# Two zero columns on three products of each block of 24

## The chip, the cores and the metric

The kernel runs on one core of a Trainium2 chip. What is measured is the time of one execution on the device, in microseconds. TensorE (PE in the profile, with its weight loads on a row of their own, PEld) multiplies; VectorE (DVE), ScalarE (ACT) and GpSimd (POOL) do the element-wise work; SyncE (SP) issues the transfers.

## The reference

Two transformer blocks on 256 tokens of width 1024, batch 1, in float32. The parts that matter here are the plain matrix products:

```python
def first_block(x, c, positions, w_ada, ...):
    ...
        proj = xn @ w_in[l]
        ...
        mixed = g_moba * (o_moba @ w_proj_moba[l]) + g_rwkv * (o_rwkv @ w_proj_rwkv[l])
        h = h + gt1 * (mixed @ w_out[l])
        xn2 = rms_norm(h, norm2_g[l]) * (1.0 + sc2) + sh2
        h = h + gt2 * peer_ffn(xn2, peer_wq[l], peer_subkeys[l], peer_u[l], peer_v[l])
...
def retrieve(args):                       # in peer_ffn
    ...
        hdn = jax.nn.gelu(jnp.einsum('cd,chkd->chk', xc, uc).astype(jnp.float32), approximate=False) * gc
        return jnp.einsum('chk,chkd->cd', hdn.astype(vc.dtype), vc)
...
def hybrid_layer(...):                    # second block: attention, then
    ...
    x = x + gate_f * ((jax.nn.silu(gt) * val) @ w_down)
```

The kernel computes the retrieval densely: all 16,384 experts' hidden values, with the gates of the chosen ones, and all their outputs.

## The kernel before, in words

**Products.** Every weight matrix is cut into units of 128 partitions by 1024 numbers, 512 KB each. `raw` loads a unit, and `wsplit` splits it into a rounded part `hi` (ScalarE, line 304) and the rest `lo` (VectorE, line 306), both in the type fp32r. The moving side is split in the same way into `xh` and `xl` (or `Hh` and `Hl`). A product of two float32 matrices then is three products: hi with xh, hi with xl, lo with xh. `mm3` writes them: first, for each of eight terms, hi·xh (line 322) and hi·xl (line 323), then eight times lo·xh (line 325). So a unit is a **block of 24** TensorE products, each with a weight load of 128x128 and 256 moving columns (the tokens).

**Two kinds of blocks.** In `t_unit` the eight terms are the eight rows k of `xh` (128 features each), and all 24 products add up in one PSUM tile `mmo`. In the two places with the outputs spread over 1024 columns (the experts' outputs, tiles `acc`, 128 units; the second block's down projection, tiles `facc`, 22 units), the eight terms are eight slices of the weights, the moving rows are one `Hh` and `Hl`, and each product adds into its own half of one of four PSUM tiles that stay open over all units.

**Stages in order of time.** The opening (to about 73 us) computes the first norm row by row and multiplies each row as it comes (`z`, lines 699 and 703). Then come the two mixers of block 1, its output projection (`wout` in `block1_out`, from 303 us), the query projection and the experts' hidden values (`u_pair`: two units into one PSUM tile; once the routing is known, from 550 us on, 16 small fp16 products `pg` follow most pairs), the experts' outputs (783 to 1141 us), block 2's mixer, its output projection (tiles `mh`, `ml`), and the feed-forward (1411 us to the end). At three of the norms `norm_apply` multiplies the first two units row by row (lines 457 and 465) while the rows are computed.

**Order.** All engines run their own instruction lists in order; the scheduler of the language layer has set that order at build time, from priorities and its own estimate of when operands are there. The waits are semaphores. `shim` allocates and clears small tiles so that the following tiles start at chosen addresses.

Of the kernel before, what the change touches and what calls it, by code (L numbers as in the profile page):

```python
# [269 lines left out]
class Prog:  # L270
    def __init__(self, tc, a, wu, cc, dbg=None, upto=99):
# [4 lines left out]
        self.nshim = 0  # L276
# [50 lines left out]
    def t_unit(self, u, xh, xl, kc=8):  # L327
        hi, lo = self.wsplit(u)
        hi, lo = hi.rearrange("p (k n) -> p k n", k=kc), lo.rearrange("p (k n) -> p k n", k=kc)
        ps = self.mm.tile([128, T], F32, name="mmo", tag="mm")  # L330
        A = slice(None)
        self.mm3([(ps, (A, k, slice(0, 128)), (A, k), k == 0, k == kc - 1) for k in range(kc)], hi, lo, xh, xl)
        return ps
# [297 lines left out]
    def block1_mixer(self):  # L631
# [5 lines left out]
        xh = bp.tile([128, 8, T], F32R, name="xh")  # L637
        xl = bp.tile([128, 8, T], F32R, name="xl")
# [401 lines left out]
    def block1_out(self):  # L1040
# [5 lines left out]
        xh = bp.tile([128, 8, T], F32R, name="xh")  # L1046
        xl = bp.tile([128, 8, T], F32R, name="xl")
# [19 lines left out]
    def peer(self):  # L1067
# [26 lines left out]
        xh = xp.tile([128, 8, T], F32R, name="xh")  # L1094
        xl = xp.tile([128, 8, T], F32R, name="xl")
# [127 lines left out]
        def u_pair(i):  # L1223
            ps = self.mm.tile([128, 2, T], F32, name="mmo", tag="mm")
            for j in range(2):
                hi, lo = self.wsplit(wu["u"] + i + j)
                hi, lo = hi.rearrange("p (k n) -> p k n", k=8), lo.rearrange("p (k n) -> p k n", k=8)
                A = slice(None)
                self.mm3([(ps[:, j], (A, k), (A, k), j == 0 and k == 0, k == 7) for k in range(8)], hi, lo, xh, xl)
# [90 lines left out]
        acc = [pa.tile([128, 2, T], F32, name=f"acc{i}") for i in range(4)]  # L1320
        from itertools import chain
        self.bg = chain(self.ada("ada1", "c", "b1", self.mod1, (5,), 24), self.ada("ada2", "c2", "b2", self.mod2, range(6)))
        for i in range(128):
            hi, lo = self.wsplit(wu["v"] + i)
            with tc.high_priority(self.lead + 12):
                Hh = vp.tile([128, T], F32R, name="Hh", bufs=4)
                Hl = vp.tile([128, T], F32R, name="Hl", bufs=4)
                self.split(hslice(i // 2 * 2)[:, i % 2], Hh, Hl)
            A = slice(None)
            self.mm3([(acc[d // 2][:, d % 2], (A, slice(d * 128, (d + 1) * 128)), A, i == 0 and d % 2 == 0, i == 127) for d in range(8)], hi, lo, Hh, Hl,  # L1330
                     inner=(i == 127))
# [19 lines left out]
    def block2_mixer(self):  # L1351
# [16 lines left out]
        xh = bp.tile([128, 8, T], F32R, name="xh")  # L1368
        xl = bp.tile([128, 8, T], F32R, name="xl")
# [345 lines left out]
    def ffn(self):  # L1715
# [4 lines left out]
        with ExitStack() as st:  # L1720
# [7 lines left out]
            xh = bp.tile([128, 8, T], F32R, name="xh")  # L1728
            xl = bp.tile([128, 8, T], F32R, name="xl")
# [8 lines left out]
            def up(i):  # L1738
# [12 lines left out]
                Hh = rp.tile([128, T], F32R, name="Hh", tag="Hh")  # L1751
# [36 lines left out]
```

## Time and profile before

| | |
|---|---|
| median of 3 runs | 1605.67 us (1603.52 to 1613.95) |
| the profiled execution, its own time | 1610.28 us |
| its span, first to last instruction | 1608.0 us |
| mean granted clock of TensorE | 0.996 |
| TensorE busy | 97% of the span, 13,022 products |
| VectorE, ScalarE busy | 79%, 63% |

A profile shows one execution, here the one with 1610.28 us: 4.6 us above the median of the other runs and inside their range. Busy time of TensorE is modelled from the starts of its products; since products overlap in the array, a single product is listed with some 0.28 us although the next one starts 0.11 to 0.12 us after it. What the engine delivers is read from the starts.

### The profile page before, as it was taken

Reading aid. Unit: us, or ns where it says so; the run is one execution under the profiler, and the core shown is the slowest. Engines: PE = TensorE matmul, PEld = TensorE weight load, DVE = VectorE, ACT = ScalarE, POOL = GpSimd, SP = SyncE. Lnnn points to the kernel's source line nnn. Section 1 sums busy time; section 2 is a strip of 40 time slices with the busy share of each in tenths; the row PEclk is TensorE's granted clock in tenths of the full one; section 3 lists DMA queues with packets and bytes.
Section 4 is the critical chain, followed back from the end, with each engine's and each line's share of the span. In section 5 each row is a group of like instructions: output and inputs, shape, how many; then the busy total and the mean of one; then the engine's idle time right before and its main releaser. Section 6 shows DMA issues by size and latency. Waiting matters only on the chain.

```text
span 1608.0 us, 33360 instructions
## 1 busy us (share of the span) xinstructions
PE 1562.9 (97%) x13022; PEld 1504.4 (94%) x13022; DVE 1263.5 (79%) x2731; ACT 1019.4 (63%) x2093; POOL 6.5 (0%) x43
## 2 busy tenths in 40 slices
PE   5999999999999999999999999999999999999998
PEld 5888898989999999999999999999888998989998
DVE  7887887878789777888877777777798986777776
ACT  4475765555545799998654445444679786665553
POOL 0000000000000000000000000000000000000000
PEclk8999999999999999999999999999999999999999
DMA  8632336645544544444688878788666322435553
GB/s 308 247 106 93 119 128 225 231 141 179 183 166 170 184 161 169 169 159 171 212 275 274 274 261 278 269 287 271 203 211 224 133 87 102 168 121 186 190 189 105
DMA packets 85261, 306.63 MB, mean 191 GB/s; under 512 B 9456, under 2 KB 10992, under 8 KB 84976
## 3 DMA queue, kind: packets, MB, share of 16 engines
q1 hardware_dynamic: 85104, 304.51, 55.4%
q8 instruction: 102, 1.67, 0.4%
q14 instruction: 55, 0.45, 0.1%
HBM read 303.42 MB, written 1.05 MB: 189 GB/s over the span
## 4 chain that ended last, share of the span: by engine, by line
PE 85%; DVE 8%; ACT 3%; DMA 2%; issue 1%; SPq 0%; DVEq 0%; ACTq 0%
PE mmo L322 14%; PE mmo L325 14%; PE mmo L323 14%; PE acc L322 7%; PE acc L323 7%; PE acc L325 7%; DVE lo L306 3%; DMA raw<-w 2%; PE pg L1263 2%; PE facc L322 1%; PE facc L325 1%; PE facc L323 1%; ACT hi L304 1%; PE pxt L893 1%; PE pz L881 1%
## 5 line engine op out<-in xcount | busy, mean ns | idle before, releaser
L304 ACT ACTIVATE hi<-raw 128x1024 fp32r<-128x1024 f32 (+1 forms) x465 | 490.4, 1057 | 370.0 <-PE mmo L323 136.1
L306 DVE TENSOR_TENSOR lo<-raw,hi 128x1024 fp32r<-128x1024 f32 (+1 forms) x465 | 565.2, 1218 | 165.7 <-ACT hi L304 162.6
L322 PE MATMUL mmo<-xh,hi 128*128 128x256 f32 x2032 | 498.8, 286 | 1.6 <-ACT hi L304 0.6
L323 PE MATMUL mmo<-xl,hi 128*128 128x256 f32 x2032 | 490.4, 281 | 0.0
L322 PEld LDWEIGHTS mmo<-xh,hi 128*128 128x128 f32 x2032 | 382.8, 189 | 5.7 <-ACT hi L304 2.1
L323 PEld LDWEIGHTS mmo<-xl,hi 128*128 128x128 f32 x2032 | 383.3, 189 | 1.9 <-issue 0.2
L325 PE MATMUL mmo<-xh,lo 128*128 128x256 f32 x2032 | 283.3, 281 | 4.7 <-DVE lo L306 4.6
L325 PEld LDWEIGHTS mmo<-xh,lo 128*128 128x128 f32 x2032 | 255.6, 189 | 7.2 <-DVE lo L306 6.5
L322 PE MATMUL acc<-Hh,hi 128*128 128x256 f32 x1024 | 241.8, 278 | 0.5 <-ACT Hh L363 0.5
L323 PE MATMUL acc<-Hl,hi 128*128 128x256 f32 x1024 | 241.0, 278 | 0.0
L322 PEld LDWEIGHTS acc<-Hh,hi 128*128 128x128 f32 x1024 | 192.3, 188 | 0.7 <-ACT Hh L363 0.7
L323 PEld LDWEIGHTS acc<-Hl,hi 128*128 128x128 f32 x1024 | 192.5, 188 | 0.1
L325 PE MATMUL acc<-Hh,lo 128*128 128x256 f32 x1024 | 139.4, 277 | 0.0
L325 PEld LDWEIGHTS acc<-Hh,lo 128*128 128x128 f32 x1024 | 127.3, 188 | 0.0
L388 DVE SCALAR_TENSOR_TENSOR acc<-raw,sil,acc 128x1024 f32<-128x1024 f32 x70 | 89.8, 1283 | 44.8 <-DMA raw<-w 44.7
L1245 ACT ACTIVATE D<-iota,i 128x128 f16<-128x128 f16 x256 | 84.6, 404 | 0.2
L1252 DVE TENSOR_TENSOR B<-O,iT 128x512 f16<-128x512 f16 x128 | 46.1, 417 | 0.0
L323 PE MATMUL facc<-Hl,hi 128*128 128x256 f32 x176 | 42.8, 281 | 0.0
L322 PE MATMUL facc<-Hh,hi 128*128 128x256 f32 x176 | 42.8, 281 | 0.0
L364 DVE TENSOR_TENSOR Hl<-hidA,Hh 128x256 fp32r<-128x256 f32 x96 | 40.0, 418 | 0.0
L363 ACT ACTIVATE Hh<-hidA 128x256 fp32r<-128x256 f32 x96 | 38.2, 400 | 0.0
L1246 ACT ACTIVATE A<-D 128x512 f16<-128x512 f16 x64 | 37.8, 628 | 0.0
(503 smaller groups left out, 2273.3 us busy)
## 6 DMA issues: line engine op xcount, KB each, us to landing
raw<-w SPq DMA_DIRECT2D x542, 512.0 KB, 4.1
aw<-w SPq DMA_DIRECT2D x16, 512.0 KB, 7.3
raw<-w SPq DMA_DIRECT2D x6, 384.0 KB, 3.3
whole<-w SPq DMA_DIRECT2D x4, 512.0 KB, 7.2
c<-w SPq DMA_DIRECT2D x3, 512.0 KB, 6.2
x<-xT SPq DMA_DIRECT2D x2, 512.0 KB, 5.7
hres<-xT SPq DMA_DIRECT2D x1, 1024.0 KB, 5.5
sk<-w SPq DMA_DIRECT2D x2, 512.0 KB, 5.6
```

What stands on the lines that cost most here:

```text
L304: self.s.activation(hi[:, :n], r[:, :n], AF.Copy)
L306: self.v.tensor_tensor(lo[:, :n], r[:, :n], hi[:, :n].bitcast(F32), OP.subtract)
L322: m(out, whi[w], xhi[x], start=start, stop=False, skip_group_check=True)
L323: m(out, whi[w], xlo[x], start=False, stop=False, skip_group_check=True)
L325: m(out, wlo[w], xhi[x], start=False, stop=stop, skip_group_check=True)
L363: self.s.activation(hi, src, AF.Copy)
L364: self.v.tensor_tensor(lo, src, hi.bitcast(F32), OP.subtract)
L388: v.scalar_tensor_tensor(acc, w, sc, acc, OP.mult, OP.add)
L1245: s.activation(D[:, j], iota, AF.Abs, bias=i1[:, t0 + j:t0 + j + 1])
L1246: s.activation(A, D, AF.Relu, scale=-1.0, bias=1.0)
L1252: v.tensor_tensor(B[p], O, row(1 + p), OP.mult)
L1263: mm(pg[:, j], B[p][:, :, j], A[:, j], start=(j + p == 0), stop=(j == 3 and p == 1), skip_group_check=True)
```

## The change

Each moving tile gets 64 more columns behind its last row, which GpSimd clears once (`rows`). In the blocks that use such a tile, three of the 24 products take 258 moving columns instead of 256: the last row and two of the zeros behind it. Their output is two columns wider, so that the zeros are added to two columns beyond the product's own, which are either unused (in `t_unit` the PSUM tile is two columns wider) or the beginning of the other half of the tile.

So that the wide products stand eight apart, `unit` starts each block with row 7 (hi·xh), puts hi·xl of row 7 in the ninth place and lo·xh of row 7 in the seventeenth. In `u_pair` the first unit of each pair has the wide products. `spread` does the same for `acc` and `facc` in the places 1, 9 and 17 of each block (slices 0 and 4 with hi, slice 0 with lo), all with the same moving row `Hh`; the last block is without. The four `Hh` tiles are now named ones, used in turn. The blocks that `t_units` writes, the second block's output projection (`mh`, `ml`) and the products of the opening and the norms keep 256 columns.

In all, 190 blocks of `mmo` (three in `xh`/`xl` each), 127 of `acc` and 21 of `facc` have wide products: 338 blocks, 1,014 products.

```diff
+    def rows(self, pool, k, name, **kw):
+        t = pool.tile([128, k * T + 64], F32R, name=name, **kw)
+        self.g.memset(t.bitcast(F32)[:, k * T:], 0.0)
+        x = t[:, :k * T].rearrange("p (k n) -> p k n", k=k)
+        return x, t[:, (k - 1) * T:k * T + 2]
+
+    def unit(self, ps, wide, hi, lo, xh, xl, kc, start=True):
+        tails, A, q = self.tails.get(id(xh)), slice(None), slice(0, 128)
+        ops = [(w, x, k) for k in range(kc) for w, x in ((hi, xh), (hi, xl))]
+        low = [(lo, xh, k) for k in range(kc)]
+        if tails and wide is not None and kc == 8:
+            a, b = ops[-2:]
+            ops = [a] + ops[:7] + [b] + ops[7:-2]
+            low = low[-1:] + low[:-1]
+        else:
+            tails = None
+        ops += low
+        for n, (w, x, k) in enumerate(ops):
+            if tails and k == kc - 1:
+                out, mv = wide, tails[0 if x is xh else 1]
+            else:
+                out, mv = ps, x[:, k]
+            self.pe.matmul(out, w[:, k, q], mv, start=start and n == 0, stop=n == len(ops) - 1, skip_group_check=True)
...
+    def spread(self, acc, hi, lo, Hh, Hl, wide, first, last):
+        C = lambda d: slice(d * 128, (d + 1) * 128)
+        if last:
+            ops = [(d, w, x) for d in range(8) for w, x in ((hi, Hh), (hi, Hl), (lo, Hh))]
+        else:
+            ops = [(d, w, x) for d in range(8) for w, x in ((hi, Hh), (hi, Hl))] + [(d, lo, Hh) for d in range(8)]
+        for n, (d, w, x) in enumerate(ops):
+            out = acc[d // 2][:, d % 2]
+            if n % 8 == 0 and not last:
+                out, x = acc[d // 2].rearrange("p j n -> p (j n)")[:, :T + 2], wide
+            self.pe.matmul(out, w[:, C(d)], x, start=first and d % 2 == 0 and w is hi and (n % 2 == 0), stop=last and w is lo, skip_group_check=True)
...
-        xh = bp.tile([128, 8, T], F32R, name="xh")
-        xl = bp.tile([128, 8, T], F32R, name="xl")
+        (xh, a), (xl, b) = self.rows(bp, 8, "xh"), self.rows(bp, 8, "xl")
+        self.tails[id(xh)] = a, b
...
-                self.mm3([(ps[:, j], (A, k), (A, k), j == 0 and k == 0, k == 7) for k in range(8)], hi, lo, xh, xl)
+                wide = ps.rearrange("p j n -> p (j n)")[:, :T + 2] if j == 0 else None
+                self.unit(ps[:, j], wide, hi, lo, xh, xl, 8, j == 0)
```

How the order of TensorE's instructions moves is seen at three places. The first is any block of the experts' outputs, here the first half of one. Before:

```order
L322 MATMUL acc_10720<-Hh,hi 128x256
L323 MATMUL acc_10720<-Hl,hi 128x256
L322 MATMUL acc_10720<-Hh,hi 128x256
L323 MATMUL acc_10720<-Hl,hi 128x256
L322 MATMUL acc_10721<-Hh,hi 128x256
L323 MATMUL acc_10721<-Hl,hi 128x256
L322 MATMUL acc_10721<-Hh,hi 128x256
L323 MATMUL acc_10721<-Hl,hi 128x256
L322 MATMUL acc_10722<-Hh,hi 128x256
```

Now, from the second product of a block on, to the ninth:

```order
L371 MATMUL acc_10726<-Hl,hi 128x256
L371 MATMUL acc_10726<-Hh_10734,hi 128x256
L371 MATMUL acc_10726<-Hl,hi 128x256
L371 MATMUL acc_10727<-Hh_10734,hi 128x256
L371 MATMUL acc_10727<-Hl,hi 128x256
L371 MATMUL acc_10727<-Hh_10734,hi 128x256
L371 MATMUL acc_10727<-Hl,hi 128x256
L371 MATMUL acc_10728<-Hh_10734,hi 128x258
```

Nothing has moved here; the first and the ninth product have 258 columns.

The second place is TensorE at the beginning of block 1's output projection. The products with `orh` and `orl` are the last of the branch projections, out of which `xh` is still being made, row by row up to row 7. Before, the first `wout` unit begins with row 0:

```order
L322 MATMUL mmo<-orh,hi 128x256
L323 MATMUL mmo<-orl,hi 128x256
L325 MATMUL mmo<-orh,lo 128x256 x4
L322 MATMUL mmo<-xh,hi 128x256
L323 MATMUL mmo<-xl,hi 128x256
L322 MATMUL mmo<-xh,hi 128x256
L323 MATMUL mmo<-xl,hi 128x256
```

Now, with row 7 first:

```order
L348 MATMUL mmo<-orh,hi 128x256
L349 MATMUL mmo<-orl,hi 128x256
L351 MATMUL mmo<-orh,lo 128x256 x4
L313 MATMUL mmo<-xh,hi 128x258
L313 MATMUL mmo<-xh,hi 128x256
L313 MATMUL mmo<-xl,hi 128x256
L313 MATMUL mmo<-xh,hi 128x256
L313 MATMUL mmo<-xl,hi 128x256
```

All products of the first units, which stood before those that need row 7, stand behind one that needs it.

The third place is TensorE at the end of the opening, before the last of its eight rows (products `z`). Before, 22 products of the next stage (`mmo`) stand between the seventh and the eighth row:

```order
L699 MATMUL z_122<-xh,lo 128x256 x2
L699 MATMUL z_123<-xh,lo 128x256 x2
L322 MATMUL mmo<-xh,hi 128x256
L323 MATMUL mmo<-xl,hi 128x256
L322 MATMUL mmo<-xh,hi 128x256
L323 MATMUL mmo<-xl,hi 128x256
```

Now the eighth row follows at once (the names z are counted two higher):

```order
L737 MATMUL z_124<-xh,lo 128x256 x2
L737 MATMUL z_125<-xh,lo 128x256 x2
L737 MATMUL z_122<-xh,hi 128x256 x2
L737 MATMUL z_123<-xh,hi 128x256 x2
L737 MATMUL z_124<-xh,hi 128x256 x2
L737 MATMUL z_125<-xh,hi 128x256 x2
```

The 22 products have moved behind the `z` of row 7, where all 48 of the next stage now stand together. In the same way, at the three norms with `norm_apply`, the places between the rows held 7 or 8 products of other units than the small ones and now hold 6.

## Rows read from the trace of the kernel before

**Rows 1.** The page, parts 1 and 4: busy times and the chain by engine

```profile
PE 1562.9 (97%) x13022; PEld 1504.4 (94%) x13022; DVE 1263.5 (79%) x2731; ACT 1019.4 (63%) x2093; POOL 6.5 (0%) x43
...
PE 85%; DVE 8%; ACT 3%; DMA 2%; issue 1%; SPq 0%; DVEq 0%; ACTq 0%
```

**Rows 2.** The page, part 5: one group of the feed-forward, busy and mean ns

```profile
L323 PE MATMUL facc<-Hl,hi 128*128 128x256 f32 x176 | 42.8, 281 | 0.0
```

**Rows 3.** Timeline, TensorE, experts' outputs: block starts 16 blocks apart (start, us, engine)

```profile
986.99 0.28 PE L322 MATMUL acc<-Hh,hi 128*128 128x256 f32 x1
...
1030.51 0.28 PE L322 MATMUL acc<-Hh,hi 128*128 128x256 f32 x1
```

**Rows 4.** Timeline, TensorE, an earlier stretch there: block starts 16 blocks apart

```profile
885.48 0.28 PE L322 MATMUL acc<-Hh,hi 128*128 128x256 f32 x1
...
930.70 0.28 PE L322 MATMUL acc<-Hh,hi 128*128 128x256 f32 x1
```

**Rows 5.** Windows, TensorE: stretch, length, busy (products), clock, DMA share, GB/s

```profile
388.91:407.40 18.49, 18.49 (x159) 1.00 0.43 148
...
494.68:515.63 20.95, 20.95 (x180) 1.00 0.45 155
883.00:933.00 50.00, 50.00 (x427) 1.00 0.80 268
1034.00:1085.00 51.00, 51.00 (x436) 1.00 0.82 279
...
1431.00:1600.00 169.00, 169.00 (x1437) 1.00 0.49 169
```

**Rows 6.** Timeline, TensorE, two pairs of hidden-value units with gate products between

```profile
551.41 0.28 PE L322 MATMUL mmo<-xh,hi 128*128 128x256 f32 x1
...
555.89 1.10 PE L325 MATMUL mmo<-xh,lo 128*128 128x256 f32 x8
...
557.93 0.28 PE L323 MATMUL mmo<-xl,hi 128*128 128x256 f32 x1
558.05 0.28 PE L322 MATMUL mmo<-xh,hi 128*128 128x256 f32 x1
...
558.28 0.28 PE L322 MATMUL mmo<-xh,hi 128*128 128x256 f32 x1
...
562.37 1.07 PE L325 MATMUL mmo<-xh,lo 128*128 128x256 f32 x8
```

**Rows 7.** Groups by line, TensorE: 985 to 1033 us, then block 2's mixer (1141 to 1391)

```profile
L323 PE MATMUL acc<-Hl,hi 128*128 128x256 f32 x142 | 33.1, 276 | 0.0
...
L325 PE MATMUL mmo<-xh,lo 128*128 128x256 f32 x288 | 39.5, 279 | 0.0
```

**Rows 8.** Timeline at the end of the opening: TensorE and, ahead of row 7, ScalarE

```profile
62.68 0.28 PE L322 MATMUL mmo<-xh,hi 128*128 128x256 f32 x1
...
64.17 0.51 ACT L438 ACTIVATE xh<-nt,mod 128x256 fp32r<-128x256 f32 x1 [3.53 <-DVE nt L437]
...
65.27 0.40 PE L699 MATMUL z<-xh,hi 128*128 128x256 f32 x2
```

**Rows 9.** Timeline at the start of block 1's output projection: TensorE and ScalarE

```profile
303.44 0.28 PE L322 MATMUL mmo<-xh,hi 128*128 128x256 f32 x1
...
306.65 0.50 PE L323 MATMUL mmo<-xl,hi 128*128 128x256 f32 x2
306.97 0.42 ACT L363 ACTIVATE xh<-gt 128x256 fp32r<-128x256 f32 x1 [1.72 <-DVE gt L1054]
307.44 0.51 PE L322 MATMUL mmo<-xh,hi 128*128 128x256 f32 x2 [0.28 <-ACT xh L363]
```

**Rows 10.** Windows, all engines, at the norm of 327 us (columns as in rows 5)

```profile
326.00:331.00 5.00, 2.33 (x12) 1.43 (x12) 3.17 (x6) 3.31 (x8) 0.00 (x0) 1.00 0.62 210
331.00:335.00 4.00, 4.00 (x18) 3.53 (x17) 2.92 (x8) 2.52 (x7) 0.00 (x0) 0.57 0.02 9
```

**Rows 11.** Timeline, TensorE, the same norm: a product put between the rows

```profile
331.58 0.42 PE L322 MATMUL mmo<-xh,hi 128*128 128x256 f32 x1
```

More of the change, by code (lines that the diff above doesn't have):

```diff
@@ L329, in t_unit @@
         hi, lo = hi.rearrange("p (k n) -> p k n", k=kc), lo.rearrange("p (k n) -> p k n", k=kc)
[L330 to L333, printed above, removed]
+        ps = self.mm.tile([128, T + 2], F32, name="mmo", tag="mm")
+        self.unit(ps[:, :T], ps, hi, lo, xh, xl, kc)
+        return ps[:, :T]
+    def spread(self, acc, hi, lo, Hh, Hl, wide, first, last):
[9 more added lines that the diff above has]
+            self.pe.matmul(out, w[:, C(d)], x, start=first and d % 2 == 0 and w is hi and (n % 2 == 0), stop=last and w is lo, skip_group_check=True)
     def t_units(self, hi, lo, kc, nbs, xh, xl, n, where=None):
@@ L1045, in block1_out @@
         sy.dma_start(h, self.a["xT"])
-        xh = bp.tile([128, 8, T], F32R, name="xh")
-        xl = bp.tile([128, 8, T], F32R, name="xl")
+        (xh, a), (xl, b) = self.rows(bp, 8, "xh"), self.rows(bp, 8, "xl")
+        self.tails[id(xh)] = a, b
         for j in range(4):
@@ L1320, in peer @@
         acc = [pa.tile([128, 2, T], F32, name=f"acc{i}") for i in range(4)]
+        Hhs = [(x[:, 0], w) for x, w in (self.rows(vp, 1, f"Hh{i}", tag=f"Hh{i}", bufs=1) for i in range(4))]
         from itertools import chain
@@ L1324, in peer @@
             hi, lo = self.wsplit(wu["v"] + i)
+            (Hh, wide), Hl = Hhs[i % 4], vp.tile([128, T], F32R, name="Hl", bufs=4)
             with tc.high_priority(self.lead + 12):
-                Hh = vp.tile([128, T], F32R, name="Hh", bufs=4)
-                Hl = vp.tile([128, T], F32R, name="Hl", bufs=4)
                 self.split(hslice(i // 2 * 2)[:, i % 2], Hh, Hl)
-            A = slice(None)
-            self.mm3([(acc[d // 2][:, d % 2], (A, slice(d * 128, (d + 1) * 128)), A, i == 0 and d % 2 == 0, i == 127) for d in range(8)], hi, lo, Hh, Hl,
-                     inner=(i == 127))
+            self.spread(acc, hi, lo, Hh, Hl, wide, i == 0, i == 127)
             if i == 4:
@@ L1367, in block2_mixer @@
         self.shim(ep, AT_B2)
[L1368 to L1369 removed]
+        (xh, a), (xl, b) = self.rows(bp, 8, "xh"), self.rows(bp, 8, "xl")
+        self.tails[id(xh)] = a, b
         M = lambda i: self.mod2[:, 8 * i:8 * i + 8]
@@ L1727, in ffn @@
             self.shim(rp, AT_FF)
-            xh = bp.tile([128, 8, T], F32R, name="xh")
-            xl = bp.tile([128, 8, T], F32R, name="xl")
+            (xh, a), (xl, b) = self.rows(bp, 8, "xh"), self.rows(bp, 8, "xl")
+            self.tails[id(xh)] = a, b
             self.shim(bp, 256 - AT_FF)
@@ L1755, in up, with down @@
                 self.split(val, Hh, Hl)
-                return Hh, Hl
-            def down(i, Hh, Hl):
+                return Hh, Hl, wide
+            def down(i, Hh, Hl, wide):
                 hi, lo = self.wsplit(wu["down"] + i)
-                A = slice(None)
-                self.mm3([(acc[d // 2][:, d % 2], (A, slice(d * 128, (d + 1) * 128)), A, i == 0 and d % 2 == 0, i == 21) for d in range(8)], hi, lo, Hh, Hl,
-                         inner=(i == 21))
+                self.spread(acc, hi, lo, Hh, Hl, wide, i == 0, i == 21)
+            Hhs = [(x[:, 0], w) for x, w in (self.rows(rp, 1, f"Hh{i}", tag=f"Hh{i}", bufs=1) for i in range(4))]
             hid = {}
```

10 lines of the change are left out of this document (4 added, 6 removed).

## The prediction

> **What bounds the kernel now.** I read part 1 of the page and its chain first: TensorE is busy 97% of the span and holds 85% of the chain that ended last [rows 1]. So nearly every nanosecond between two products is on the path, and the question is how fast products follow each other. The busy times don't tell that, since products overlap; the starts do. I went through TensorE's timeline, stage by stage, and looked at the distance between starts within long sequences of 256-column products.
>
> There are two steps, and almost nothing between. In one stretch of the experts' outputs 16 blocks of 24 products take 1030.51 - 986.99 = 43.52 us, 113.3 ns a product [rows 3]. In an earlier stretch, with the same instructions, 16 blocks take 930.70 - 885.48 = 45.22 us, 117.8 ns [rows 4]. I call them the short and the long step; they differ by 4.4 ns. The clock row says 1.00 in both [rows 5], so the clock, at its level of 2.4 GHz, isn't the difference, and TensorE waits for no other engine in either. A stretch keeps its step until something else comes between (transposes, the fp16 gate products, a wait) and is then drawn anew: of seven long stretches of the experts' outputs two have the long step, and the feed-forward has it from end to end, 1437 products in 169 us [rows 5], 117.6 ns with the records at the edges counted in.
>
> In cycles of 2.4 GHz the short step is 272 for 256 columns, the long one 282.6, near 282 2/3. That isn't a whole number: if the long step is the mean of a fixed pattern, the pattern is one over three products (848 cycles). So with the short step every product stands alike, with the long one there seem to be three places.
>
> **The change part by part: the wide products.** Two columns more are 0.83 ns at 2.4 GHz. Adding up columns, 1,014 wide products cost 1,014 x 0.83 = 0.8 us. The bounds: the short step leaves 113.3 - 106.7 = 6.7 ns beyond its 256 columns, in which two may vanish, so 0; at the other end, the longest ordinary step that I find near a stretch is the 0.12 us from 557.93 to 558.05 [rows 6], 6.7 ns above the short step, so 1,014 x 6.7 = 6.8 us. I take 0.8, since the slack is eight times the pad.
>
> **The Trainium skill on this.** The page "TensorE: Matmul & The Clock Gate", section "Back-to-back issue gap", gives a step of the columns at 2.4 GHz plus 2.5 ns: 109.2 ns for 256 columns, 110.0 for 258, and knows one step alone. The trace disagrees: 113.3 and 117.8. By the page each pad is lost time and there is no step to win; that is the second rival below.
>
> **What the pads can win.** A pad moves the following start by a fraction of a step. With the long step, places 1, 9 and 17 of a block fall on all three places of a three-product pattern (eight apart is two places on), so one of the three pads meets whichever place can be pushed over. If the short step swallows a pad in its slack and the long one doesn't, every stretch with the long step turns to the short one within a block, and stays so.
>
> What is there to win: long steps in blocks that get pads. Feed-forward 1,437, almost the whole stage, whose mean 281 ns goes with the long step [rows 2, 5]. Experts' outputs: two of seven stretches, 427 and 436 products [rows 5], together 863. Hidden values from 550 us: of each two pairs one has the long step, 38 of them from 551.41 to 555.89 (117.9 ns), one the short, 36 from 558.28 to 562.37 (113.6) [rows 6]; this repeats 18 times until 777 us, with some 46 long steps each: 828. From 342 to 550 us four stretches, the first of 159 and the last of 180 products [rows 5], 579 in all. Block 2's mixer: its lo·xh products have a mean of 279 ns between 276 (short step) and 281 (long) [rows 2, 7]; of about 860 products some 60%, 500. Together 4,200 x 4.4 ns = 18.7 us. Before 342 us I count nothing; it would be 1 us at most.
>
> Not all is won. Each newly drawn stretch keeps the long step until the right pad, ten products on average, and in the pairs the second block has no pads. 25 stretches (1, 2, 18 and 4) x 10 x 4.4 ns = 1.1 us, and in the mixer, with stretches of about 20 products, half of 2.2 us is lost. **Gain: 18.7 - 2.2 = 16.5 us.**
>
> **Row 7 first.** This moves work past a wait, in three kinds of places.
> - Output projection of block 1: before, 28 products with rows 0 to 6 run from 303.44 to 306.65, while row 7 is computed; ScalarE ends it at 306.97 + 0.42 = 307.39, and TensorE goes on at 307.44 [rows 9]. Now the first product needs row 7: TensorE stands from 303.44 to 307.4, and the 28 products come after, 28 x 0.1133 = 3.2 us later than before. Nothing hides this; the later blocks are queued behind it in order.
> - Opening: 22 products filled 62.68 to 65.27 while the opening's row 7 was computed; that row is ready at 64.17 + 0.51 = 64.68 [rows 8]. Now TensorE waits till 64.7, goes on 0.6 us earlier than before, but has 22 x 0.118 = 2.6 us to make up: 2.0 us lost.
> - The three norms: the products between the rows fall from 7 or 8 to 6, some 4 each, which filled waits such as that at 331.58 [rows 11]: 3 x 4 x 0.113 = 1.3 us at most; I take 1.3 (0 if the rows come sooner for it).
>
> Then the clock: at the norm of 327 us TensorE was busy 2.33 of 5 us, and in the 4 us after that the granted clock was 0.57, that is 1.2 GHz for most of it, and 18 products ran [rows 10], where at the short step 35 would fit: some 1.7 us lost, as those there weren't all bound by TensorE. The new wait of 4.0 us at 303 us is an unbroken one; I count 1.7 us for it (0 if the clock holds).
>
> **The rest.** 18 small memsets on GpSimd, which is busy 6.5 us of the span [rows 1], take their time beside other work; if a first block waited for its zeros, a fraction of a microsecond. Four named Hh tiles in the place of a pool's four or three move no wait that I see.
>
> **Sum.** -16.5 + 0.8 + 3.2 + 2.0 + 1.3 + 1.7 = -7.5 us. Against the profiled execution's own 1610.28 that is 1602.8; this execution lies 4.6 us above the median, and the steps may have been drawn differently in the others. I apply the difference to the median: 1605.67 - 7.5 = **1598.2 us**. About 1% (16 us) is what a measurement of this kernel can tell from no change.
>
> **The rivals.**
> 1. *The pads throw the short step out as well.* If a wide product among short steps leaves the next start outside the place that the short step needs, each pad draws anew, and with three places of the long step to one of the short, about three quarters of the 9,600 steps in these blocks would be long, 7,200 for 4,200: 3,000 x 4.4 = 13.2 us lost, plus the 9.0 us of costs: 1605.7 + 22 = 1628 us. It speaks for it that disturbances do switch the step, and both ways (the two alternate from pair to pair [rows 6]); against it, the 6.7 ns of slack. It decides if the share of long steps doesn't fall: the costs are covered only from 9.0 / 0.0044 = 2,050 long steps fewer.
> 2. *The pads do nothing*: both steps take two columns in their slack and go on. Then the costs alone stand: 1605.7 + 9.0 = 1614.7 us. It speaks for it that the long step has even more slack (117.8 - 106.7 = 11 ns); against it, that something in it must depend on where a product stands.
> 3. *The long steps go, but each pad costs 6.7 ns*: 1,014 x 6.7 = 6.8 us in the place of 0.8: 1604 us. For it speaks the step of 0.12 us; against it, that this one stands next to a disturbance.
>
> **How the numbers follow.** Forecast (long steps turn short, pads nearly free) 0.53; rival 1: 0.16; rival 2: 0.20; rival 3: 0.11. The forecast's own range: without the clock loss, the norms' and the pads' cost, and with an immediate turn, -7.5 - 1.7 - 1.3 - 0.8 - 2.2 = -13.5, 1592 us; if only two thirds of the gain come, 1604 us. With the spread of the times before (1603.5 to 1614) I go from 1589 to 1619, which takes in rivals 2 and 3 and leaves out most of rival 1 and the tail below. Faster by over 1% (below 1589.6): a quarter of the forecast's cases, 0.13. Slower by over 1% (above 1621.7): rival 1 and little else, 0.15. The rest, 0.72.
>
> **What would show it.** In the profile after: the feed-forward's 256-column products with a mean of 276 ns for 281, block starts 2.72 us apart in all seven stretches of the experts' outputs, the alternation of the pairs gone; the wide products' own steps at 114 ns or less (120 for rival 3). A wait of some 4 us of TensorE for ScalarE's `xh` at 303 us, one of 2 us at 63 us, and perhaps a stretch of low clock after the first. Rival 1 shows as quick alternation with means between 279 and 281, rival 2 as unbroken stretches of 281 as before. The prediction is wrong if those stay, or if the short step isn't the floor and products with pads run faster than 113.3 ns.

## The result, and the profile after

The changed kernel takes 1624.84 us (median of 8 runs, 1622.13 to 1629.45), the one before on the same chips 1613.47 us: a ratio of 1.0092, interval 1.0073 to 1.0111. One slow execution of the kernel before, of 1997.02 us, stands in its median (1613.03 us without it) and not in the ratio, which is taken from the fast executions and is not the quotient of the two medians. The forecast was 1598.2 us; the measured time lies above its range, 1589 to 1619 us, too. The profiled execution has a span of 1620.3 us against 1608.0, that is 12.3 us more.

The page of the changed kernel, parts 1, 4 and 5; the first two lines answer to [rows 1], the last to [rows 2] (in part 5 the numbers at the end are us of busy time, mean ns of one product, and idle us before them):

```profile
PE 1569.2 (97%) x13022; PEld 1510.7 (93%) x13022; DVE 1264.8 (78%) x2731; ACT 1021.1 (63%) x2093; POOL 8.3 (1%) x61
...
PE 85%; DVE 9%; ACT 2%; DMA 2%; issue 1%; SPq 0%; DVEq 0%; ACTq 0%
...
L371 PE MATMUL acc<-Hl,hi 128*128 128x256 f32 x1024 | 244.2, 279 | 0.2 <-DVE Hl L402 0.2
...
L371 PE MATMUL facc<-Hl,hi 128*128 128x256 f32 x176 | 42.3, 279 | 0.0
```

TensorE bounds the kernel as before. The feed-forward's mean fell from 281 to 279 ns, not to the 276 ns of the short step; that of the experts' outputs stands at 279 ns too, where the short step has 276 [rows 7]. Both stages are now a mixture. The windows of the changed kernel for the two stretches of the experts' outputs in [rows 5] (columns as there, with every engine's busy time):

```profile
883.00:933.00 50.00, 50.00 (x433) 50.00 (x432) 37.42 (x48) 24.57 (x36) 0.00 (x0) 1.00 0.80 272
1034.00:1085.00 51.00, 51.00 (x441) 51.00 (x440) 39.17 (x52) 24.47 (x36) 0.83 (x9) 1.00 0.85 284
```

433 and 441 products where an all-long stretch had 427 and 436, and an all-short one would have 441 and 450: half of each. What the mixture is made of is seen in the timeline of one block and the start of the next (start, duration, engine, line, names, shape):

```profile
810.66 0.28 PE L371 MATMUL acc<-Hh,hi 128*128 128x258 f32 x1
...
811.58 0.28 PE L371 MATMUL acc<-Hh,hi 128*128 128x258 f32 x1
...
812.52 1.08 PE L371 MATMUL acc<-Hh,lo 128*128 128x258 f32 x8
813.44 0.28 PE L371 MATMUL acc<-Hh,hi 128*128 128x258 f32 x1
```

The wide products stand 0.92, 0.94 and 0.92 us apart. Eight short steps are 0.907 us, eight long ones 0.942. The wide product at 810.66 meets the long step, and after two or three transitional steps the short one runs; that at 811.58 meets the short step, and the seven behind it are long; that at 812.52 turns back. So a wide product doesn't end the long step, it **turns the step over**, whichever runs. A whole period can be read over a longer way:

```profile
897.97 1.10 PE L371 MATMUL acc<-Hh,lo 128*128 128x258 f32 x8
...
903.55 1.10 PE L371 MATMUL acc<-Hh,lo 128*128 128x258 f32 x8
```

48 products take 5.58 us, 16 of them 1.860. Eight short and eight long steps are 1.849 (8 x 113.3 + 8 x 117.8 ns), so two wide products cost 11 ns beyond that, some 5.6 ns each.

The second difference is at 303 us, where block 1's output projection begins, [rows 9] before. The changed kernel's timeline there, and windows of TensorE (length, busy, products, granted clock, DMA share, GB/s):

```profile
302.88 0.62 PE L351 MATMUL mmo<-orh,lo 128*128 128x256 f32 x4
307.74 0.56 PE L313 MATMUL mmo<-xh,hi 128*128 128x258 f32 x1 [4.24 <-ACT xh L401]
```
```profile
303.00:308.00 5.00, 0.76 (x6) 0.82 0.73 258
308.00:312.00 4.00, 4.00 (x20) 0.50 0.34 116
312.00:316.00 4.00, 4.00 (x32) 0.88 0.07 10
```

TensorE stands 4.24 us for ScalarE's row 7, and after that the granted clock is at 0.50, the 1.2 GHz level, for more than 4 us: 20 products where the kernel before has 36. The same windows of the kernel before:

```profile
303.00:308.00 5.00, 4.72 (x37) 1.00 0.82 281
308.00:312.00 4.00, 4.00 (x36) 1.00 0.32 101
312.00:316.00 4.00, 4.00 (x38) 1.00 0.77 261
```

At the end of the opening TensorE waits for row 7 too, [rows 8] before. The waits of TensorE from 60 to 304 us in the changed kernel (us in total, times, longest):

```profile
PE z L737 <- ACT xh L476: 1.9, 1, 1.9
```

The first product of the following transposes starts 2.4 us later than before (75.10 us for 72.72), but the last branch product of block 1's mixer at 303.22 us, 0.1 us earlier. So in this pair of executions the loss is given back within the mixer; in six_once and natural_two below, which have no such wait, that product starts at 305.19 and 305.42 us, so the mixer alone moves by 2 us from kernel to kernel.

### The profile page after: what moved, and what is told of

Its sections match the earlier page's. It is cut to its first block, busy times and chain, and to the rows that moved or that the text cites. A ratio compares the mean times of both kernels' runs of the same rounds, so it can differ in the third digit from the quotient of the medians.

```text
span 1620.3 us, 33392 instructions
## 1 busy us (share of the span) xinstructions
PE 1569.2 (97%) x13022; PEld 1510.7 (93%) x13022; DVE 1264.8 (78%) x2731; ACT 1021.1 (63%) x2093; POOL 8.3 (1%) x61
## 4 chain that ended last, share of the span: by engine, by line
PE 85%; DVE 9%; ACT 2%; DMA 2%; issue 1%; SPq 0%; DVEq 0%; ACTq 0%
PE mmo L313 40%; PE acc L371 22%; PE facc L371 4%; DVE lo L332 3%; PE pg L1301 2%; PE pz L919 1%; PE pxt L931 1%; DMA raw<-w 1%; ACT hi L330 1%; PE mmo L495 1%; PE z L737 1%; DVE res L1225 1%; DVE aacc L712 1%; PE ptp L549 1%; PE po L556 1%
## 5 line engine op out<-in xcount | busy, mean ns | idle before, releaser
L313 PE MATMUL mmo<-xh,hi 128*128 128x258 f32 (+1 forms) x2032 | 488.3, 287 | 4.8 <-ACT xh L401 4.2
L313 PE MATMUL mmo<-xl,hi 128*128 128x256 f32 x2032 | 470.2, 282 | 0.0
L313 PEld LDWEIGHTS mmo<-xh,hi 128*128 128x128 f32 x2032 | 372.0, 189 | 9.2 <-issue 4.9
L313 PEld LDWEIGHTS mmo<-xl,hi 128*128 128x128 f32 x2032 | 371.3, 189 | 1.0
L313 PE MATMUL mmo<-xh,lo 128*128 128x258 f32 x2032 | 284.6, 281 | 4.9 <-DVE lo L332 4.7
L371 PE MATMUL acc<-Hh,hi 128*128 128x256 f32 (+1 forms) x1024 | 245.0, 280 | 0.7 <-POOL Hh L292 0.7
L371 PE MATMUL acc<-Hh,lo 128*128 128x256 f32 (+1 forms) x1024 | 141.0, 279 | 0.0
L371 PE MATMUL facc<-Hh,hi 128*128 128x256 f32 (+1 forms) x176 | 42.3, 279 | 0.0
```

The lines of the kernel that those rows point to most:

```text
L313: self.pe.matmul(out, w[:, k, q], mv, start=start and n == 0, stop=n == len(ops) - 1, skip_group_check=True)
L371: self.pe.matmul(out, w[:, C(d)], x, start=first and d % 2 == 0 and w is hi and (n % 2 == 0), stop=last and w is lo, skip_group_check=True)
```

## The experiments

**Theory A:** each product of 258 columns turns the step over, from either one, for some 5.6 ns; the row-7 wait and the low clock behind it come on top. **Rivals:** C, a wide product only draws the step anew, without a rule; D, the prediction's three places, of which a wide product meets the right one or doesn't; and that the new order alone makes the loss. Diffs are against the changed kernel, and ratios against the kernel before on the same chip.

**order_alone**: row 7 first, everywhere 256 columns.

```diff
-        return x, t[:, (k - 1) * T:k * T + 2]
+        return x, t[:, (k - 1) * T:k * T]
...
-                out, x = acc[d // 2].rearrange("p j n -> p (j n)")[:, :T + 2], wide
+                out, x = acc[d // 2].rearrange("p j n -> p (j n)")[:, :T], wide
...
```

> The changed kernel with all products back at 256 columns; row 7 stays first and the moving tiles keep their 64 more columns. Theory A (each wide product turns the step over, from 113.3 to 117.8 ns or back, and row 7 first costs a wait and a stretch of low clock): the wait of 4.2 us at 303 us and the low clock after it stay, some 6 us from the last branch product to the norm; in the experts' outputs the steps are in long unbroken stretches again, with the mean of the hi-lo products at 276 or 281 ns by stretch; time 4 to 8 us above the kernel before, ratio 1.002 to 1.005. Theory B (the wide products are harmless, the row order and its waits cost all): 11 us above, ratio 1.007, like the changed kernel.

1617.13 us, ratio 1.0023 (1.0000 to 1.0047), as theory A has it: the order alone makes only a part of the loss. Its windows of TensorE in two of the long stretches show one that is long and one that is short without a break, and the wait remains in its list of waits:

```profile
789.00:839.00 50.00, 50.00 (x427) 1.00 0.81 264
891.00:939.00 48.00, 48.00 (x426) 1.00 0.84 277
```
```profile
PE mmo L313 <- ACT xh L401: 3.8, 1, 3.8
```

So the half-and-half mixture is the wide products' doing. 50 us with 427 products are all long, as 883 to 933 us were before [rows 5]; 48 us with 426 are all short. The short one is the third long stretch of the stage, and the third was at the long step before with the same instructions: which step an unbroken stretch has is not fixed by its own instructions.

**spread_alone**: wide products only in `acc` and `facc`, natural order elsewhere. The line is taken out at all five places where it stands.

```diff
-        self.tails[id(xh)] = a, b
```

> Wide products only in the 127 + 21 blocks of the experts' outputs and the down projection; all blocks of mmo as in the kernel before. Theory A (each wide product turns the step over): no wait at 303 us; the experts' outputs alternate every 8 products, 16 products in 1860 ns, so that this stage is 4 to 6 us longer than before; the feed-forward, with three wide products in 72, is a mix of the two steps, some 3 us shorter than all long. Together within 4 us of the kernel before, ratio 1.000 to 1.003. Theory B (the wide products are harmless): both stages as the steps happen to be drawn, ratio 0.998 to 1.000, no alternation.

1616.49 us, ratio 1.0011 (0.9999 to 1.0022). The experts' outputs lost 5.7 us against the profile of before and the feed-forward won 3.0: the turning over makes half of a stage long, which harms a stage that was mostly short and helps one that was all long.

**units_alone**: the other part, row 7 first and wide products only in `mmo`.

```diff
-            if n % 8 == 0 and not last:
-                out, x = acc[d // 2].rearrange("p j n -> p (j n)")[:, :T + 2], wide
```

> The wide products (2 columns) and row 7 first in the blocks of mmo alone; the experts' outputs and the down projection at 256 columns. Theory A (a wide product turns the step over, and two turns cost 1860 - 8 x 113.3 - 8 x 117.8 = 11 ns beyond the two steps): the wait and low clock at 303 us 6.2 us, 570 wide products 3.2 us, the feed-forward's up products mixed instead of all long 2 to 3 us less, the rest as drawn: 5 to 9 us above the kernel before, ratio 1.003 to 1.006. Theory B (the wait alone): 4 to 6 us, ratio 1.002 to 1.004, with long unbroken stretches.

1622.15 us, ratio 1.0059 (1.0035 to 1.0083). With spread_alone's 1.0011 that is 1.0070, a little below the whole change's interval (1.0073 to 1.0111). Here the feed-forward's `facc`, with no wide product of its own, ran at the short step from end to end, where it had been all long before [rows 2]. The group on the page, and the timeline from one block of `facc` to the next:

```profile
L369 PE MATMUL facc<-Hl,hi 128*128 128x256 f32 x176 | 41.4, 276 | 0.0
```
```profile
1452.07 0.40 PE L313 MATMUL mmo<-xh,hi 128*128 128x258 f32 x2
...
1454.87 0.40 PE L313 MATMUL mmo<-xh,hi 128*128 128x258 f32 x2
...
1457.65 0.28 PE L369 MATMUL facc<-Hh,hi 128*128 128x256 f32 x1
```

Between two blocks of `facc` stand two of `mmo` with three wide products each. Six turns are an even number, so every block of `facc` meets the step that the first one met; that this was the short one is the draw.

**probe_width**: natural order; in the experts' outputs every second block's first product is wide, by 2 to 32 columns in turn.

```diff
+WIDTHS = (2, 4, 6, 8, 10, 12, 14, 16, 2, 24, 32)
...
+                m = T + pads[n]
+                out, x = acc[d // 2].rearrange("p j n -> p (j n)")[:, :m], wide[:, :m]
```

> In every second block of the experts' outputs the first product is wide, by 2, 4, 6, 8, 10, 12, 14, 16, 2, 24, 32 columns in turn; all else as before (no wide products elsewhere). Theory A: each product wide by 2 turns the step over, from whichever it was, and the step then stays for the two blocks. For the other widths it says nothing sure, but if a grid of 16 cycles (6.67 ns) is what the steps are tied to, 16 and 32 leave the step as it is and cost 6.7 and 13.3 ns, and some width between may lead to the short step from both. Theory C (a wide product draws anew): after the same width now the short, now the long step, without rule.

1614.39 us, one run. By the starts around each wide product: 2 columns turned the step over from both sides, each of eleven times. 12 and 14 did the same, from both sides, each of six times, and 8 led from the short step to the long, six of six (never seen from the long). **6 columns led to the short step from both sides**: from the long one each of five times, from the short one the once that it met it. 10 led from the long to the short, six of six (never seen from the short). 16 led from either to the short, though a few longer steps stand in between; 4, 24 and 32 went either way. So no simple order by width shows: 6 lead to the short step, and 12 and 14 turn it over again. The timeline of this kernel at two products of 262 columns, the first met in the long step, the second in the short:

```profile
796.30 1.10 PE L383 MATMUL acc<-Hh,lo 128*128 128x256 f32 x8
797.24 0.28 PE L383 MATMUL acc<-Hh,hi 128*128 128x262 f32 x1
...
797.61 0.28 PE L383 MATMUL acc<-Hl,hi 128*128 128x256 f32 x1
...
798.40 0.28 PE L383 MATMUL acc<-Hh,hi 128*128 128x256 f32 x1
...
1045.81 1.07 PE L383 MATMUL acc<-Hh,lo 128*128 128x256 f32 x8
1046.72 0.28 PE L383 MATMUL acc<-Hh,hi 128*128 128x262 f32 x1
...
1048.09 0.28 PE L383 MATMUL acc<-Hh,hi 128*128 128x256 f32 x1
```

Ahead of the first, eight products take 0.94 us, and behind it, from 797.61, seven take 0.79 (113 ns). Ahead of the second, eight take 0.91, and from it on twelve take 1.37, only 10 ns more than short steps would. A free draw (C) would not go the same way each time; for 2, 6, 12 and 14 columns it falls. For 4, 24 and 32 a draw isn't excluded.

**probe_pairs**: likewise, but with two products of 258 columns in such a block, 2 to 18 places apart.

```diff
+PAIRS = ((0, 4), (0, 8), (0, 12), (0, 16), (0, 18), (16, 18), (16, 22))
```

> In every second block of the experts' outputs two products are wide by 2 columns, 4, 8, 12, 16, 18, 2 or 6 products apart; all else as before. Theory A in its plain form (each wide product turns the step over, wherever it falls): after two the step is the one before, at every distance. Theory D (as in the prediction: the long step is a pattern over three products, and only one of its three places can be pushed over): from the short step, distances with the same remainder by 3 end alike, 8 (and 2 and 18, 16 by their remainders 2, 0 and 1) showing one remainder that comes back to the short step and others that stay long.

1614.76 us, one run. From the short step every pair, at each of the seven distances, came back to the short step: the second product took back what the first had done. From the long one the pairs came back to the long, with one exception, which theory A in its plain form didn't expect: two products two apart, met in the long step, ended in the short one three of four times. The timeline of this kernel for the pair four apart:

```profile
785.67 1.07 PE L383 MATMUL acc<-Hh,lo 128*128 128x256 f32 x8
786.58 0.28 PE L383 MATMUL acc<-Hh,hi 128*128 128x258 f32 x1
...
787.05 0.28 PE L383 MATMUL acc<-Hh,hi 128*128 128x258 f32 x1
...
787.65 0.28 PE L383 MATMUL acc<-Hl,hi 128*128 128x256 f32 x1
...
787.99 0.28 PE L383 MATMUL acc<-Hh,hi 128*128 128x256 f32 x1
```

From 787.65 to 787.99 three steps take 0.34 us, 113 ns each: the short step is back. With three places (D) the outcome from the short step would hang on the distance; it doesn't. Two states explain these pairs, and a turn between them takes a few products: a second wide product inside it need not turn back.

**six_for_two**: the changed kernel with 6 zero columns in the place of 2.

```diff
-        return x, t[:, (k - 1) * T:k * T + 2]
+        return x, t[:, (k - 1) * T:k * T + 6]
...
-                out, x = acc[d // 2].rearrange("p j n -> p (j n)")[:, :T + 2], wide
+                out, x = acc[d // 2].rearrange("p j n -> p (j n)")[:, :T + 6], wide
```

> The changed kernel with 6 columns in the place of 2 on the same 1,014 products. Theory E (from the widths tried: 6 columns lead to the short step from both): the long step is gone from these blocks within a block; a wide product among short steps costs about 7 ns in it and the two behind it (117, 115, 115), 1,014 x 7 = 7 us; the wait at 303 us stays, 6 us; gain against the kernel before some 19 us: 1600 to 1612, ratio 0.993 to 0.999. Theory A (any pad turns the step over, the width aside): as the changed kernel, ratio 1.009.

1611.14 us, ratio 0.9995 (0.9977 to 1.0014), a little above what was expected. Only the width is changed, and the whole loss is gone (ratio 1.0092 with 2 columns); the wait at 303 us and the low clock remain.

**spread_six**: one product of 262 columns per block (the ninth), in `acc` and `facc` alone, natural order.

```diff
-            if n % 8 == 0 and not last:
+            if n == 8 and not last:
-                out, x = acc[d // 2].rearrange("p j n -> p (j n)")[:, :T + 2], wide
+                out, x = acc[d // 2].rearrange("p j n -> p (j n)")[:, :T + 6], wide
...
```

> One wide product of 6 columns (the ninth) in each block of the experts' outputs and the down projection; blocks of mmo as before. Theory E (6 columns lead to the short step): both stages all short, 3.9 us and 6.5 us gained, 147 x 7 ns = 1.0 us paid: 8 to 10 us below the kernel before, ratio 0.994 to 0.996. Theory A (any pad turns the step over): the experts' outputs half long, 1 to 3 us above, ratio 1.001.

1605.90 us, ratio 0.9958 (0.9937 to 0.9979): inside the ratio that theory E gives, though 6.7 us below the median of the kernel before are a little less than the 8 to 10 us stated with it.

**six_once**: one such product per block in all the blocks of the change; `mmo` in natural order (the pairs take row 7 third), so no wait at 303 us.

```diff
+        ks = (0, 1, 7, 2, 3, 4, 5, 6) if early else range(kc)
+        ops = [(w, x, k) for k in ks for w, x in ((hi, xh), (hi, xl))]
...
+            if tails and k == kc - 1 and w is hi and x is xh:
+                out, mv = wide, tails[0]
...
+            if n == 8 and not last:
+                out, x = acc[d // 2].rearrange("p j n -> p (j n)")[:, :T + 6], wide
...
```

> One wide product of 6 columns in each block that can have one: the ninth in the experts' outputs and the down projection, hi.xh of row 7 in the blocks of mmo, with the rows in their own order (row 7 third in the hidden-value pairs, eighth elsewhere), so that no product is moved past the wait for row 7 at 303 us. Theory E (6 columns lead to the short step): no wait there; in mmo some two thirds of the long steps go, 8 to 10 us less 1.3 us for 190 wide products, with the two other stages 15 to 18 us below the kernel before, ratio 0.989 to 0.991. Theory A (any pad turns the step over): within 3 us of the kernel before.

1602.09 us, ratio 0.9939 (0.9917 to 0.9961): faster than both kernels, by somewhat less than expected. Wide products of consecutive blocks in its timeline, eleven blocks between the first and the last:

```profile
984.95 0.28 PE L368 MATMUL acc<-Hh,hi 128*128 128x262 f32 x1
...
1014.94 0.28 PE L368 MATMUL acc<-Hh,hi 128*128 128x262 f32 x1
```

A block takes (1014.94 - 984.95) / 11 = 2.726 us, 24 short steps 2.720: the wide product costs some 6.5 ns and keeps the short step.

**six_first**: six_once with row 7 first in the blocks that are not of a pair. The step is short nearly everywhere in both, so this prices the order.

```diff
+        if tails and not early:
+            ops = ops[-2:-1] + ops[:-2] + ops[-1:]
```

> The kernel of six_once (one product of 262 columns per block) with row 7 first in the blocks that are not of a pair, so that the first product of block 1's output projection needs row 7 again; the step is the short one nearly everywhere in both, so that this prices the order alone. Theory: a wait of some 4 us at 303 us, then the granted clock at 0.5 for 3 to 7 us, together 5 to 7 us there, and up to 2 us at the end of the opening: 0.9939 + 0.0035 to 0.0055 = 0.9974 to 0.9994 of the kernel before. Rival (the order weighs 2 us or less, as order_alone's 1.0023 could also be read): 0.993 to 0.9955.

1607.53 us, ratio 0.9977 (0.9955 to 0.9999), as theory has it. That is 5.4 us more than six_once by the medians, which come from two chips; by the ratios, each to the kernel before on its own chip, it is 0.0038, some 6 us. Its list of waits and its windows of TensorE (six_once has 44 and 29 products there, both at a clock of 1.00):

```profile
PE mmo L312 <- ACT xh L400: 4.2, 1, 4.2
```
```profile
303.00:308.00 5.00, 0.75 (x8) 0.83 0.85 312
308.00:312.00 4.00, 4.00 (x19) 0.50 0.35 124
```

**natural_two**: the changed kernel with all rows in natural order, so that `mmo`'s wide products stand in places 15, 16 and 24.

```diff
-            a, b = ops[-2:]
-            ops = [a] + ops[:7] + [b] + ops[7:-2]
-            low = low[-1:] + low[:-1]
...
```

> The changed kernel with its 1,014 wide products, but all rows in natural order: in the blocks of mmo the wide products stand in places 15, 16 and 24, and no block starts with row 7. Theory (the loss has three parts that add up: the step turned over, the row-7 wait, the low clock behind it): the wait of 4.2 us at 303 us is gone, and with it the 6.8 us at the granted clock of 0.5, together 6.3 us between the last branch product and the norm, while the turning over stays, and means of 279 to 280 ns with it: 1.0092 - 6.3 / 1613 = 1.0053 times the kernel before (1.003 to 1.007). Rival (the waiting time is filled elsewhere, since order_alone came out at 1.0023 only, so the wait weighs 2 us or less): 1.008 or more. A third, that places 15 and 16 side by side don't turn the step over twice: mmo's long steps then fall or rise as a whole, and the time leaves 1.003 to 1.009 on either side.

1623.13 us, ratio 1.0086 (1.0055 to 1.0118): the main expectation missed. The wait is gone, as the windows show:

```profile
303.00:308.00 5.00, 5.00 (x42) 1.00 0.88 292
308.00:312.00 4.00, 3.63 (x28) 1.00 0.75 268
```

Up to the next norm it is 3.2 us ahead of the changed kernel, but this is lost again by the end. The third possibility of the expectation holds: side by side, two wide products don't turn the step twice, as two of them two places apart mostly didn't in probe_pairs. In the timeline of `mmo` blocks, places 15 and 16 met in the long step end in the short one, with a few steps of 120 to 124 ns between, and place 24 turns to the long again, in which the next block starts; some two thirds of such a block are long, not half. Summed over `mmo`, the time beyond the short step is 19.8 us, against 16.8 in the changed kernel. This kernel's profile also has the granted clock at 0.50 at 51, 1205 and 1427 us. The order is therefore priced by six_first, not here.

**narrow**: a probe of what holds the step. Natural order, no wide products; in the experts' outputs the products take only the first 254, 252, ... 128 of the 256 columns, six blocks at each width, and leave out the rest, so that the output is incomplete.

```diff
+            m = WIDTHS[(i - 1) // 6 % 20] if 0 < i < 121 else T
+            self.spread(acc, hi, lo, Hh, Hl, i == 0, i == 127, m)
```

> The kernel before in the blocks of mmo; in the experts' outputs the products of blocks 1 to 120 take only the first 254, 252, 250, 248, 246, 244, 240, 236, 232, 228, 224, 216, 208, 200, 192, 176, 160, 144, 128 and 250 of the 256 columns, six blocks each, so the other columns of the experts' outputs are left out. It measures the step against the columns. Theory F (the slack of the prediction: something other than the columns, of fixed length, holds the short step at 113.3 ns): the step stays at 113.3 ns down to some width, and no long step remains once the columns are few. Theory G (the columns and a fixed surcharge make the step): it falls by 0.83 ns for each 2 columns, to 60 ns at 128. Theory H (the steps are tied to a grid of 6.67 ns): plateaus of whole multiples, or mixes of such, 106.7 to 113.3 between 240 and 254 columns.

1764.51 us, one run: slower with less work, for a reason beside the question. TensorE got ahead of its weights, as its waits say (us in total, times, longest), and the granted clock fell to 0.50 again and again:

```profile
PE acc L371 <- DVE lo L334: 70.7, 30, 4.7
```

Between the waits the step can still be read. Timeline at the start of a block and of the next, for 250, 144 and 128 columns, and windows of TensorE there:

```profile
839.95 0.28 PE L371 MATMUL acc<-Hh,hi 128*128 128x250 f32 x1
...
842.83 0.28 PE L371 MATMUL acc<-Hh,hi 128*128 128x250 f32 x1
...
1197.67 0.41 PE L371 MATMUL acc<-Hh,hi 128*128 128x144 f32 x1
...
1202.79 0.41 PE L371 MATMUL acc<-Hh,hi 128*128 128x144 f32 x1
...
1225.88 0.27 PE L371 MATMUL acc<-Hh,hi 128*128 128x128 f32 x1
...
1228.56 0.27 PE L371 MATMUL acc<-Hh,hi 128*128 128x128 f32 x1
```
```profile
840.00:842.50 2.50, 2.50 (x23) 1.00 0.89 336
1225.00:1228.50 3.50, 3.50 (x34) 1.00 0.79 246
1193.00:1217.00 24.00, 24.00 (x114) 0.50 0.32 111
```

At a clock of 1.00, 24 products of 128 columns take 2.68 us, 111.7 ns each: half the columns, and 1.6 ns less than the short step. A block of 192 columns has the same 111.7 ns. At 0.50, the 1.2 GHz level, 24 products of 144 columns take 5.12 us, 213.3 ns each, and every width from 128 to 254 that was met at this clock has this step. So something other than the number of moving columns holds the step, and it nearly doubles when the clock halves. Theory G falls (60 ns at 128 columns). Nor does the step fall steadily on the way down: at 250 columns it is 2.88 us / 24 = 120.0 ns, longer than either step at 256, in each of the five blocks of this width that no wait broke, while at 252, in the one block without a wait, it is 113.3 again. So H falls too (106.7 to 113.3 ns between 240 and 254 columns), and of F the fixed floor is left, not its level of 113.3 ns.

The Trainium skill, page "TensorE: Matmul & The Clock Gate", section "LDWEIGHTS (loading the stationary operand)", gives a weight load of 128 columns a time of columns / 1.2 GHz, 106.7 ns by an estimate from it. The measured floor of 111.7 ns lies near, every product here has a load of its own, and the 213.3 ns at the low clock are twice that estimate, though the formula makes no difference by the clock; no run here shows that the load is what holds the step.

## Why the prediction was wrong

For every kernel I summed over its trace what each step between two products of one kind (`mmo`, `acc` or `facc`; those of 110 to 130 ns) lies above the short step of 113.3 ns: the time that long steps and turns cost together. "Order" is 5.5 us for row 7 first: the profiled spans of six_first and six_once differ by 6.4 us (1604.4 - 1598.0), their sums by 0.8. The last two columns set the change of the sum, with the order, against the profiled span less 1608.0.

| kernel | `mmo` | `acc` | `facc` | sum, us | change + order | measured |
|---|---|---|---|---|---|---|
| before | 16.5 | 3.9 | 2.3 | 22.6 | | |
| changed | 16.8 | 8.9 | 1.4 | 27.0 | 4.5 + 5.5 = 10.0 | 12.3 |
| order_alone | 16.1 | 5.8 | 2.3 | 24.1 | 1.6 + 5.5 = 7.1 | 9.2 |
| spread_alone | 13.2 | 8.9 | 1.4 | 23.5 | 0.9 | 4.3 |
| units_alone | 16.7 | 5.8 | 0.0 | 22.5 | -0.1 + 5.5 = 5.4 | 12.3 |
| natural_two | 19.8 | 8.9 | 1.8 | 30.4 | 7.8 | 13.1 |
| six_for_two | 8.2 | 2.9 | 0.4 | 11.4 | -11.2 + 5.5 = -5.7 | -1.5 |
| spread_six | 12.2 | 1.3 | 0.2 | 13.8 | -8.8 | -4.7 |
| six_once | 6.6 | 1.1 | 0.2 | 7.9 | -14.7 | -10.0 |
| six_first | 7.2 | 1.4 | 0.2 | 8.7 | -13.8 + 5.5 = -8.3 | -3.7 |

The signs come out right, and the order but among the four longest; for the changed kernel 2.3 us remain. But in every row 2 to 7 us more are measured than the sum says, always to the same side. A part of it can be read from the granted clock: its mean is 0.996 in the profile of before and 0.995 to 0.988 in the others. In units_alone, where the most is missing, it is at 0.50 in four places (52, 1161, 1206 and 1431 us) beside those of the wait at 303 us and of the norm behind it; the kernel before has 1.00 from 336 to 1600 us. Windows of TensorE, two of units_alone and the long one of before:

```profile
1161.50:1164.50 3.00, 3.00 (x12) 0.50 0.68 276
1206.00:1209.00 3.00, 3.00 (x14) 0.50 0.38 91
```
```profile
336.00:1600.00 1264.00, 1248.22 (x10609) 1.00 0.57 194
```

That isn't all: six_once has a mean clock of 0.995, near that of before, and lacks 4.7 us. The rest stays open.

The columns are not independent of each other, since blocks without wide products go on in the step that their neighbours leave. In the feed-forward two blocks of `mmo` stand between two of `facc`: there `mmo` has 4.0 us before, 1.9 in spread_alone and 0.0 in spread_six, with wide products in `facc` alone, and `facc` has 0.0 in units_alone. How far the draw alone goes is seen at `acc` in order_alone and units_alone: no wide products in the stage, and 1.9 us above the kernel before.

- **The step that failed** is "If the short step swallows a pad in its slack and the long one doesn't, every stretch with the long step turns to the short one within a block, and stays so", and with it the three places. A product of 258 columns throws the short step out as it does the long one, so the stages stay half long. The three places that were to make the difference aren't there: from the short step the distance of two wide products doesn't matter (probe_pairs). A gain of 16.5 us less 0.8 became a loss of 4.5 us: the feed-forward's `facc` won 0.9, the experts' outputs lost 5.0, and `mmo` as a whole stayed as it was. The pool was there: 22.6 us before, where 18.7 had been counted, and six_once takes 14.7 of it, 10.5 us by the medians (1612.58 to 1602.09).
- **The slack** was no slack for two columns: 5.6 ns a turn, for 1,014 some 5.7 us where 0.8 stood, near the upper bound of 6.8 us that rival 3 had. They are in the 27.0 us of the table; without them the long steps fell by about 1 us, not by 16.5.
- **Row 7 first at 303 us**: the mechanism was right, the size not. Wait and clock were put at 3.2 + 1.7; to the next norm the profile shows 6.25 us, since the clock stayed at the lower level for over 4 us.
- **The opening's** 2.0 us came (1.9 us of wait, the transposes 2.4 us later); whether it lasts through the mixer, the traces don't settle. The **norms'** 1.3 us can't be seen by itself. Of the **rest**, the memsets, one wait of TensorE for GpSimd's zeros is in the list of waits, 0.7 us at the experts' outputs. Priced as a whole, by six_first, the new order costs 5 to 6 us, for 3.2 + 2.0 + 1.3 + 1.7 = 8.2 in the sum.
- **The base.** The difference was put on 1605.67 us, the median of three executions; over eight the kernel before has 1613.47. Of the 26.6 us between forecast and time some 8 are this base, which has nothing to do with the change.
- **Rivals.** Rival 1 ("the pads throw the short step out as well") had the sign, the sentence and, with 1628 us, nearly the time, but a free draw behind it with three quarters long; it is a turn with half long. Its 22 us were too much for a measured 0.92%, some 15 us; that 1628 comes so near to 1624.84 is in part the luck of the low base. The sign that was named for it, quick alternation with means between 279 and 281, is what the profile shows. Its 0.16 was too little: that disturbances switch the step both ways stood in [rows 6], and the counterargument, the 6.7 ns of slack, was only a length of time, not an observation of a product that had been pushed.

What makes the two steps, and why 2 columns turn them over while 6 lead to the short one, stays open. Narrow says only that the step doesn't follow the number of moving columns.

## What to carry to other kernels

A steady loop can have two speeds with the same instructions, so read the distance between starts, not the busy time, and before a disturbance is spread over a whole kernel try it in one stage, with several sizes, from both states: here 2 columns on 1,014 products ended 0.9% above the kernel before (with the new order), 6 on the same products level with it, and 6 once a block in the old order 0.6% below. Moving the operand that is ready last to the head of TensorE's queue to set a pattern didn't pay: the wait of 4.2 us came back a second time as low clock, and the new order as a whole cost 5 to 6 us.

## What was not expected of the hardware

- The short step (113.3 ns for 256 columns) hardly falls with the columns: 111.7 ns at 128, and at 250 columns it is 120.0. At 1.2 GHz it is 213.3 ns, from 128 columns to 254.
- A product 2 columns wider turns the step over between 113.3 and 117.8 ns; one 6 columns wider ends in the short step from both, for some 6.5 ns; 12 and 14 turn it over again.
- A single wait of TensorE of 4.2 us was followed by 20 products in 4 us at a granted clock of 0.50, in place of 36.
